# Sharing the last split weights between two passes, and moving low parts of weights from GpSimd to VectorE, in a two-block float32 model kernel

## The chip, the cores and the metric

The kernel runs on one core of one Trainium2 chip. The metric is the device time of one launch in microseconds. The kernel before the change took 1829.82 us, the median of three runs (1828.95 to 1830.59). PE is the matmul engine, DVE is VectorE, ACT is ScalarE, POOL is GpSimd, and SP is the engine whose queue starts most DMAs.

## The reference

All tensors are float32; x has 256 tokens of width 1024, and so has a second sequence, ctx. A first block (chunked retention and a gated linear recurrence) makes a new x. A second block has two layers, and in layer 0 both x and ctx go through nearly all of it, with the same weights:

```python
for l in range(DEPTH_2):                        # 2 layers
    h  = modulate(rms_norm_2(x,  g_pre_mix[l]), sh1, sc1)
    hc = modulate(rms_norm_2(xc, g_pre_mix[l]), csh1, csc1)
    (mq, ..., aq, ak, av, nq, nk, nv, zg) = split(h @ w_in[l])      # and the same of hc
    y_ml = mlstm_branch(...)                    # both sequences
    y_ga = gqa_latent(rope(rms(q_a)), rope(rms(k_a)), v_a, kc_a, vc_a)
    y_na = na_latent(...)                       # window attention
    o = merge_branches(y_ml, y_ga, y_na, zg, w_branch[l], w_out[l])
    x = x + ga1 * rms_norm_2(o, g_post_mix[l])
    f = conv_ffn(modulate(rms_norm_2(x, g_pre_ffn[l]), sh2, sc2), w_up[l], conv_w[l], conv_b[l], w_down[l])
    x = x + ga2 * rms_norm_2(f, g_post_ffn[l])
    if not last:                                # the same for xc, with the same weights
        ...
```

## The kernel before

**Products.** Matrix products have float32 accuracy from three products of rounded parts. A weight chunk of 128x1024 (512 KB) is loaded by SP into a buffer `wr` (L104), ACT casts it to its high part `wh` (L106), and DVE, or GpSimd where the caller names it with `eng`, subtracts to get the low part `wl` (L107). There are four buffers of each kind. Then `mm3` (L123 to L125) issues three matmuls for each tile: high by high, high by low, low by high. The activations are split likewise, into `hh` and `hl` for the normalized input of a layer. The accumulators lie in PSUM: four banks with tag `g`, two with tag `t` (names `psg`, `pst`), two more for scores.

**Normalization and put.** `post` adds the normalized output of a product to the residue (L1163). `norm_scale` then has ACT sum the squares (L269), DVE computes the reciprocal root in tiny steps of 128x2 (`rstd`: L247 to L261) and scales both halves of the tokens (L272, into `o` or `u`). `put_h` and `norm_put` have PE transpose the result in 128x128 pieces (L283, sixteen in all, in four banks' worth through two banks), after which DVE and ACT apply gain and shift and split the result into `hh` and `hl` (L297 to L302).

**Order.** Each engine executes its instructions in an order that the tile scheduler settles before the launch, from the order of the program and the buffers. An instruction that waits holds everything behind it on its engine. Two sequences, x (s = 0) and ctx (s = 1), share the weights of layer 0, but in three places the kernel makes two passes over a weight, one for each sequence, so that one pass's products run while the other sequence is normalized:

- The attention `gqa` of layer 0: `keys` (w_akv, two chunks, a pass is 48 matmuls of 128x256) and `queries` (w_aq, four chunks, 48 matmuls of 128x512), for ctx (k1, q1) and for x (k0, q0). q1 calls the put of x before its last chunk. After the products each stage normalizes its heads (`heads`, `query_heads`; L760 to L791) on DVE. A list named `order` says in which sequence the stages are issued. `behind` issues a stage after the put of x.
- w_o of layer 0, in `out_proj`: the last weight is gone over for x, then `between()` normalizes x, then it is gone over for ctx. Behind it, `put_h` for x, `post(1)` for ctx, the first four up-weights (`up_w`), and `put_h` for ctx.
- w_dn of layer 0, also in `out_proj`: 22 row blocks, six chunks of 128x1024 at most, a pass is 132 matmuls. The ctx pass calls the put of x among its products, before its last two chunks.

In each of these the second pass loads, casts and splits its chunks again, and their low parts are made by GpSimd. The other uses of `eng` are in the first block.

Of the kernel before, what the change touches and what calls it, by code (L numbers as in the profile page):

```python
# [72 lines left out]
class Kern:  # L73
# [70 lines left out]
            except StopIteration as e:  # L144
                return e.value

    def gemm_tok(self, src, x, seqs, order=None, eng=None, among=None):


        pss = {s: self.bank("g", 4).rearrange("p (t c) -> p t c", t=2) for s in seqs}  # L150
        nk = src.shape[-1] // 256
        order = order or list(range(0, nk, 4))
        done = 0
        for i, k0 in enumerate(order):
            if among and i + among[0] == len(order):
                among[1]()
            hi, lo = self.weights(src[:, k0 * 256 : min(nk, k0 + 4) * 256], eng)
            hi = hi.rearrange("p (k c) -> p k c", c=256)
            lo = lo.rearrange("p (k c) -> p k c", c=256)
            m = hi.shape[1]  # L160
            for s in seqs:
                for t in range(2):
                    for j in range(m):
                        r = slice(s * T + t * P, s * T + (t + 1) * P)
                        self.mm3(pss[s][:, t], x(k0 + j, r), (hi[:, j], lo[:, j]), done + j + t == 0, done + j + 1 == nk and t == 1)
            done += m
        return pss

    def gemm_wide(self, src, x, seqs, order=None, eng=None, at=None):


        while self.cur:
            self.step()
        pss = {s: [self.bank("g", 4) for _ in range(2)] for s in seqs}
        nk = src.shape[-1] // 512
        order = order or list(range(0, nk, 2))
        for i, k0 in enumerate(order):
            if at and i in at:
                at[i]()
            hi, lo = (a.rearrange("p (k c) -> p k c", c=512) for a in self.weights(src[:, k0 * 512 : (k0 + 2) * 512], eng))  # L180
            for s in seqs:
                for t in range(2):
                    for j in range(2):
                        r = slice(s * T + t * P, s * T + (t + 1) * P)
                        self.mm3(pss[s][t], x(k0 + j, r), (hi[:, j], lo[:, j]), i + j == 0, i + 1 == len(order) and j == 1)
        return pss
# [546 lines left out]
    def gqa(self, l, qs, fills):  # L733
        nc, A = self.nc, self.A
        y = self.new_y(len(qs) * T)
        with ExitStack() as es:
# [73 lines left out]
            vt, qT = {}, {}  # L810
            kT = [self.tl(gp, [P, 2, 512], "akT", 2, F32R) for _ in range(2)]

            def keys(qs):
                pss = self.gemm_tok(A[f"w_akv{l}"][0], self.h, qs, eng=nc.gpsimd if l == 0 else None)
                split = {}
                yield
                for s in qs:
                    vt[s] = self.tl(gp, [P, 2, P], "av", 2)
                    nc.scalar.copy(vt[s], pss[s][:, :, P:T])
                for s, k in zip(qs, heads([pss[s][:, :, 0:P] for s in qs], 2, qs, 1)):  # L820
                    ks = split[s] = self.tl(gp, [P, 8, 2, 64], "hs", 3, F32R).rearrange("p (h a) c f -> p h (a c) f", a=2)
                    for c in range(2):
                        nc.scalar.copy(ks[:, :, c], k)
                    for c in range(2):
                        nc.vector.tensor_tensor(ks[:, :, 2 + c], k, ks[:, :, c].bitcast(F32), ALU.subtract)
                yield
                for s, ks in split.items():
                    for kv in range(2):
                        pt = self.bank("t", 2)
                        for c in range(2):  # L830
                            for tt in range(2):
                                src = ks[:, 2 * tt + kv, 2 * c : 2 * c + 2].bitcast(F32).rearrange("p c f -> p (c f)")
                                nc.tensor.transpose(pt[:, c * T + tt * P : c * T + (tt + 1) * P], src, self.idn)

                        nc.scalar.copy(kT[kv][:, :, s * T : (s + 1) * T], pt.rearrange("p (c t) -> p c t", c=2))
                yield

            def queries(s, among=None):
                pss = self.gemm_wide(A[f"w_aq{l}"][0], self.h, (s,), eng=nc.gpsimd if l == 0 else None, at=among)[s]
                sts = []  # L840
                yield
                for q in query_heads((s, pss)):
                    st = self.tl(gp, [P, 8, 2, 64], "hs", 3, F32R)
                    nc.scalar.copy(st[:, :, 0], q)
                    nc.vector.tensor_tensor(st[:, :, 1], q, st[:, :, 0].bitcast(F32), ALU.subtract)
                    sts.append(st)
                yield
                for pr in range(4):
                    pt = self.bank("t", 2)
                    for j in range(2):  # L850
                        for tt in range(2):
                            src = sts[tt][:, 2 * pr + j].bitcast(F32).rearrange("p c f -> p (c f)")
                            nc.tensor.transpose(pt[:, j * T + tt * P : j * T + (tt + 1) * P], src, self.idn)
                    qT[s, pr] = self.tl(gp, [P, 2, T], "aqT", 4 * len(qs), F32R)
                    nc.scalar.copy(qT[s, pr].rearrange("p c t -> p (c t)"), pt)
                yield


            def put(ys, s):
                self.low = self.put_h(ys, l, 0, s)  # L860
                yield

            def behind(stage):
                with self.tc.issue_after(self.low):
                    next(stage)
                yield

            def fill(us):
                self.fill(us)
                yield  # L870

            if l == 0:
                k1, q1, k0, q0 = keys((1,)), queries(1, {3: lambda: next(put(self.yx, 0))}), keys((0,)), queries(0)
                order = (k1, q1, k0, behind(k1), q1, k1, q0, k0, q1, q0, k0, fill(fills[0]), q0)
            else:
                q0, k = queries(0), keys((0, 1))
                order = (q0, put(self.yc, 1), fill(2.5), q0, k, q0, k, fill(fills[0]), k)
# [305 lines left out]

    def out_proj(self, ws, x, qs, put, between, **among):

        c = 0
        for g, (w, n) in enumerate(ws):
            gemm = self.gemm_wide if n == 512 else self.gemm_tok
            cs = slice(c, c + n)
            c += n  # L1190
            pss = gemm(w, x, qs[:1] if g + 1 == len(ws) else qs)
            for s in pss:
                put(pss[s], s, g, cs)
        between()
        if len(qs) > 1:
            put(gemm(w, x, (1,), eng=self.nc.gpsimd, **among)[1], 1, g, cs)

    def layer(self, l, qs, out):
        nc, A, tc = self.nc, self.A, self.tc
# [2 lines left out]
        with ExitStack() as es:  # L1202
# [37 lines left out]
            f = FILLS[l]  # L1240
# [25 lines left out]
            def post(s):  # L1266
# [3 lines left out]
                self.norm_scale(xs, pp, ys)  # L1270
                return ys

            def take(ps, s, g, c):
                self.take(ps, o[s], ss[s], l, 0, s, g, c)
                self.fetch([w for w in late if not w.loaded][: 6 if l else 3])

            n = {}
            self.out_proj(
                [(A[f"w_o{l}"][g], 512) for g in range(2)],
                lambda kt, r: (mh[:, kt, r], ml[:, kt, r]),  # L1280
                qs,
# [13 lines left out]
                nc.vector.scalar_tensor_tensor(u3[:, :, 1:], p3[:, :, : T - 1], cw[:, 0, n : n + 1], u3[:, :, 1:], ALU.mult, ALU.add)  # L1295
                nc.vector.scalar_tensor_tensor(u3[:, :, : T - 1], p3[:, :, 1:], cw[:, 2, n : n + 1], u3[:, :, : T - 1], ALU.mult, ALU.add)  # L1296

            def up_w(n, eng=None):
                return self.weights(A[f"w_up{l}"][n], eng)

            def new_u():
                u = self.tl(self.up, [P, 1024], "u", 2)
# [3 lines left out]
            if len(qs) > 1:  # L1306
                rest, self.fillers = self.fillers, late
                self.fill(1.0)
                self.put_h(n[0], l, 1, 0)
                yc = post(1)  # L1310
                for i in range(2):
                    us = new_u()
                    ws = [up_w(i, nc.gpsimd), up_w(22 + i, nc.gpsimd)]
                    for j in range(2):
                        up(ws[j], i + 22 * j, us[j], 0, T)
                    ahead[i] = (us, ws)
                self.drain()
                self.fillers += rest
                self.put_h(yc, l, 1, 1)
            else:  # L1320
                self.fillers += late + self.tail
                while any(not w.done for w in late):
                    self.step()
                self.put_h(n[0], l, 1, 0)
        with ExitStack() as es:
# [42 lines left out]
            put = lambda ps, s, g, c: self.take(ps, f[s], ss[s], l, 1, s, g, c)  # L1368
            ws = [(A[f"w_dw{l}"][0], 512)] + [(A[f"w_dn{l}"][g], T) for g in range(2)]
            if l == 0:  # L1370
                self.out_proj(ws, x, qs, put, lambda: n.update({0: post(0, self.xd[0])}), among=(2, lambda: self.put_h(n[0], 1, 0, 0)))
                self.yc = post(1, None)
            else:
                self.out_proj(ws[:2], x, qs, put, lambda: None)
                self.finish(pp, A[f"w_dn{l}"][1], x, f[0], ss[0], res(0), out, l)
# [116 lines left out]
```

## Time and profile before

| | us |
|---|---|
| median of three runs | 1829.82 (1828.95 to 1830.59) |
| the profiled execution | 1827.0 |
| its span | 1825.2 |
| PE busy | 1750.8 (96%) |
| DVE busy | 1157.2 (63%) |
| ACT busy | 857.8 (47%) |
| POOL busy | 251.3 (14%) |
| granted TensorE clock, mean | 0.986 |

The rows are in microseconds from the start of the span. A row of a timeline has a start, a duration, the engine, the line, the operation with its output and inputs, and a count where neighbours of one kind are put together; the bracket holds the idle time just before it on its engine and what ended that. Durations of pipelined matmuls overlap, so their spacing is read from their starts. The clock of a stretch is a share of full speed.

### The profile page before, as it was taken

To read this page: it belongs to the slowest core of one execution; us is meant where nothing else is said; L and a number is where in the kernel's file an instruction comes from. 1 tells how busy PE (TensorE), PEld (TensorE's weight loads), DVE (VectorE), ACT (ScalarE), POOL (GpSimd) and SP (SyncE) were. 2 spreads that over 40 slices of the span, in tenths; PEclk is the share of its full clock that TensorE was granted. 3 is DMA by queue.
4 is the path that set the end of the run, shared out by engine and by line. 5 is a ranking of instruction groups with operands and counts; after the bars stand their busy time and mean duration, and the time that the engine had idled before them with its cause. 6 is when DMAs were issued, how large, how long until landed. Compare 5 with 4: busy or idle time off the path is not lost. (4 is left out here: it accounts for less than half of the span.)

```text
span 1825.2 us, 28352 instructions
## 1 busy us (share of the span) xinstructions
PE 1750.8 (96%) x10776; PEld 1491.0 (82%) x10776; DVE 1157.2 (63%) x2288; ACT 857.8 (47%) x1562; POOL 251.3 (14%) x182
## 2 busy tenths in 40 slices
PE   7998987999999999998999999998999999999998
PEld 6888876777888877786877888898998987679998
DVE  7888858445434678557656564249664459768874
ACT  5463343444534545434534442235655445456652
POOL 2213042000101021003110110021001012002210
PEclk9999999999999999998999999999999999999999
DMA  8863453566534342374354324344554644576563
GB/s 304 283 204 121 136 173 109 195 205 194 191 98 156 85 130 87 132 249 161 128 185 141 102 93 134 100 142 148 166 176 148 230 128 129 202 272 200 185 222 112
DMA packets 112825, 299.11 MB, mean 164 GB/s; under 512 B 28305, under 2 KB 38609, under 8 KB 112433
## 3 DMA queue, kind: packets, MB, share of 16 engines
q1 hardware_dynamic: 111984, 296.37, 50.0%
q8 instruction: 85, 1.39, 0.3%
q10 hardware_dynamic: 432, 0.57, 0.1%
q0 software_dynamic: 272, 0.36, 0.1%
q14 instruction: 52, 0.42, 0.1%
HBM read 281.46 MB, written 19.46 MB: 165 GB/s over the span
## 5 line engine op out<-in xcount | busy, mean ns | idle before, releaser
L107 DVE TENSOR_TENSOR wl<-wr,wh 128x1024 fp32r<-128x1024 f32 (+1 forms) x333 | 412.0, 1239 | 350.2 <-ACT wh L106 343.0
L106 ACT CAST wh<-wr 128x1024 fp32r<-128x1024 f32 x368 | 382.6, 1041 | 454.3 <-PE psg L125 173.5
L123 PE MATMUL psg<-hh,wh 128*128 128x256 f32 (+1 forms) x1712 | 570.8, 335 | 0.5 <-ACT hh L298 0.5
L124 PE MATMUL psg<-hl,wh 128*128 128x256 f32 (+1 forms) x1712 | 565.9, 331 | 0.0
L125 PE MATMUL psg<-hh,wl 128*128 128x256 f32 (+1 forms) x1712 | 564.1, 330 | 0.0
L123 PEld LDWEIGHTS psg<-hh,wh 128*128 128x128 f32 x1712 | 326.8, 191 | 46.9 <-issue 11.5
L125 PEld LDWEIGHTS psg<-hh,wl 128*128 128x128 f32 x1712 | 327.4, 191 | 30.0 <-issue 0.8
L124 PEld LDWEIGHTS psg<-hl,wh 128*128 128x128 f32 x1712 | 327.4, 191 | 27.7 <-DVE hl L292 0.2
L107 POOL TENSOR_TENSOR wl<-wr,wh 128x1024 fp32r<-128x1024 f32 (+1 forms) x35 | 82.5, 2367 | 352.8 <-ACT wh L106 352.4
L123 PE MATMUL psg<-wh,hh 128*128 128x512 f32 (+1 forms) x320 | 120.6, 377 | 7.4 <-DVE p L767 5.3
L125 PE MATMUL psg<-wh,hl 128*128 128x512 f32 (+1 forms) x320 | 119.9, 375 | 2.1 <-DVE hl L302 2.1
L124 PE MATMUL psg<-wl,hh 128*128 128x512 f32 (+1 forms) x320 | 119.7, 374 | 0.0
L1340 POOL TENSOR_TENSOR u<-u 128x512 f32<-128x512 f32 (+1 forms) x44 | 61.1, 1389 | 412.7 <-DVE u L1296 412.7
L123 PE MATMUL psg<-wh,midh 128*128 128x256 f32 (+1 forms) x364 | 117.7, 323 | 0.0
L124 PE MATMUL psg<-wl,midh 128*128 128x256 f32 (+1 forms) x364 | 117.6, 323 | 0.0
L125 PE MATMUL psg<-wh,midl 128*128 128x256 f32 (+1 forms) x364 | 117.4, 322 | 0.0
L123 PEld LDWEIGHTS psg<-wh,hh 128*128 128x128 f32 x320 | 61.2, 191 | 17.9 <-DVE p L767 5.5
L123 PEld LDWEIGHTS psg<-wh,midh 128*128 128x128 f32 x364 | 69.8, 192 | 5.2
L124 PEld LDWEIGHTS psg<-wl,midh 128*128 128x128 f32 x364 | 69.7, 192 | 5.2
L683 ACT ACTIVATE p<-pss,sm 128x512 f32<-128x512 f32 x64 | 44.0, 687 | 63.7 <-DVE sm L682 63.5
L125 PEld LDWEIGHTS psg<-wh,midl 128*128 128x128 f32 x364 | 69.7, 192 | 5.1
L125 PEld LDWEIGHTS psg<-wh,hl 128*128 128x128 f32 x320 | 61.2, 191 | 12.5 <-DVE hl L302 2.5
(305 smaller groups left out, 2705.4 us busy)
## 6 DMA issues: line engine op xcount, KB each, us to landing
wr<-in_w_up_dram SPq DMA_DIRECT2D x88, 512.0 KB, 3.6
wr<-in_w_mod_dram SPq DMA_DIRECT2D x55, 512.0 KB, 4.0
wr<-in_w_zg_dram SPq DMA_DIRECT2D x48, 512.0 KB, 4.2
wr<-in_w_in_dram SPq DMA_DIRECT2D x40, 512.0 KB, 4.4
wr<-in_w_dn_dram SPq DMA_DIRECT2D x25, 512.0 KB, 3.8
wr<-in_w_br_dram SPq DMA_DIRECT2D x24, 512.0 KB, 3.6
wr<-in_w_dw_dram SPq DMA_DIRECT2D x22, 512.0 KB, 3.4
wr<-in_w_o_dram SPq DMA_DIRECT2D x20, 512.0 KB, 5.4
```

Source lines behind the costliest of these rows:

```text
L106: nc.scalar.copy(hi, raw)
L107: self.last_lo = (eng or nc.vector).tensor_tensor(lo, raw, hi.bitcast(F32), ALU.subtract).ins
L123: mm(ps, a[0], b[0], start=first, stop=False)
L124: mm(ps, a[0], b[1], start=False, stop=False)
L125: mm(ps, a[1], b[0], start=False, stop=last)
L683: nc.scalar.activation(t, s, AF.Exp, bias=m, accum_out=z)
L1340: nc.gpsimd.tensor_tensor(a, a, b, ALU.mult)
```

## The change

`parts` remembers the split parts of a chunk, and `again` gives the last ones of a pass, with the order of chunks reversed, for the next pass. Three passes use them: k0 takes both chunks of k1; q0 begins with the last two chunks of q1 and loads the other two; the ctx passes over w_o and w_dn begin with the last four chunks of the x passes, which is all of w_o, and load two of w_dn. `eng` is gone from `gemm_tok`, `gemm_wide` and `up_w`: their low parts are all made by DVE. The order of the stages in `gqa` changes, with the put of x behind the products of q1 and k1; in `out_proj` of w_o, `between()` comes behind the second pass in the program, and the take of ctx's part (`rest_put`) behind the put of x; in w_dn the put of x comes before the last chunk instead of before the last two.

```diff
@@ -144,7 +144,20 @@
             except StopIteration as e:
                 return e.value
 
-    def gemm_tok(self, src, x, seqs, order=None, eng=None, among=None):
+    def parts(self, parts, k0, src):
+
+        parts = {} if parts is None else parts
+        if k0 not in parts:
+            parts[k0] = self.weights(src)
+        return parts[k0]
+
+    @staticmethod
+    def again(parts, n=4):
+
+        ks = list(parts)[::-1]
+        return {k: parts[k] for k in ks[:n]}, ks
+
+    def gemm_tok(self, src, x, seqs, order=None, among=None, parts=None):
 
 
         pss = {s: self.bank("g", 4).rearrange("p (t c) -> p t c", t=2) for s in seqs}
@@ -154,7 +167,7 @@
         for i, k0 in enumerate(order):
             if among and i + among[0] == len(order):
                 among[1]()
-            hi, lo = self.weights(src[:, k0 * 256 : min(nk, k0 + 4) * 256], eng)
+            hi, lo = self.parts(parts, k0, src[:, k0 * 256 : min(nk, k0 + 4) * 256])
             hi = hi.rearrange("p (k c) -> p k c", c=256)
             lo = lo.rearrange("p (k c) -> p k c", c=256)
             m = hi.shape[1]
@@ -166,7 +179,7 @@
             done += m
         return pss
 
-    def gemm_wide(self, src, x, seqs, order=None, eng=None, at=None):
+    def gemm_wide(self, src, x, seqs, order=None, at=None, parts=None):
 
 
         while self.cur:
@@ -177,7 +190,7 @@
         for i, k0 in enumerate(order):
             if at and i in at:
                 at[i]()
-            hi, lo = (a.rearrange("p (k c) -> p k c", c=512) for a in self.weights(src[:, k0 * 512 : (k0 + 2) * 512], eng))
+            hi, lo = (a.rearrange("p (k c) -> p k c", c=512) for a in self.parts(parts, k0, src[:, k0 * 512 : (k0 + 2) * 512]))
             for s in seqs:
                 for t in range(2):
                     for j in range(2):
@@ -810,8 +823,8 @@
             vt, qT = {}, {}
             kT = [self.tl(gp, [P, 2, 512], "akT", 2, F32R) for _ in range(2)]
 
-            def keys(qs):
-                pss = self.gemm_tok(A[f"w_akv{l}"][0], self.h, qs, eng=nc.gpsimd if l == 0 else None)
+            def keys(qs, parts=None):
+                pss = self.gemm_tok(A[f"w_akv{l}"][0], self.h, qs, parts=parts)
                 split = {}
                 yield
                 for s in qs:
@@ -835,8 +848,9 @@
                         nc.scalar.copy(kT[kv][:, :, s * T : (s + 1) * T], pt.rearrange("p (c t) -> p c t", c=2))
                 yield
 
-            def queries(s, among=None):
-                pss = self.gemm_wide(A[f"w_aq{l}"][0], self.h, (s,), eng=nc.gpsimd if l == 0 else None, at=among)[s]
+            def queries(s, parts=None, order=None):
+                parts, order = self.again(*order) if order else (parts, None)
+                pss = self.gemm_wide(A[f"w_aq{l}"][0], self.h, (s,), order=order, parts=parts)[s]
                 sts = []
                 yield
                 for q in query_heads((s, pss)):
@@ -870,8 +884,9 @@
                 yield
 
             if l == 0:
-                k1, q1, k0, q0 = keys((1,)), queries(1, {3: lambda: next(put(self.yx, 0))}), keys((0,)), queries(0)
-                order = (k1, q1, k0, behind(k1), q1, k1, q0, k0, q1, q0, k0, fill(fills[0]), q0)
+                pk, pq = {}, {}
+                q1, k1, k0, q0 = queries(1, pq), keys((1,), pk), keys((0,), pk), queries(0, None, (pq, 2))
+                order = (q1, k1, put(self.yx, 0), k0, behind(q1), behind(k1), q0, k1, k0, q1, q0, k0, fill(fills[0]), q0)
             else:
                 q0, k = queries(0), keys((0, 1))
                 order = (q0, put(self.yc, 1), fill(2.5), q0, k, q0, k, fill(fills[0]), k)
@@ -1183,17 +1198,25 @@
 
     def out_proj(self, ws, x, qs, put, between, **among):
 
+
+        parts = {}
         c = 0
         for g, (w, n) in enumerate(ws):
             gemm = self.gemm_wide if n == 512 else self.gemm_tok
             cs = slice(c, c + n)
             c += n
-            pss = gemm(w, x, qs[:1] if g + 1 == len(ws) else qs)
+            last = g + 1 == len(ws)
+            pss = gemm(w, x, qs[:1] if last else qs, parts=parts if last else None)
             for s in pss:
                 put(pss[s], s, g, cs)
-        between()
+        if among:
+            between()
         if len(qs) > 1:
-            put(gemm(w, x, (1,), eng=self.nc.gpsimd, **among)[1], 1, g, cs)
+            parts, order = self.again(parts)
+            pss = gemm(w, x, (1,), order=order, parts=parts, **among)
+        if not among:
+            between()
+        return lambda: put(pss[1], 1, g, cs)
 
     def layer(self, l, qs, out):
         nc, A, tc = self.nc, self.A, self.tc
@@ -1270,12 +1293,13 @@
                 self.norm_scale(xs, pp, ys)
                 return ys
 
+
             def take(ps, s, g, c):
                 self.take(ps, o[s], ss[s], l, 0, s, g, c)
                 self.fetch([w for w in late if not w.loaded][: 6 if l else 3])
 
             n = {}
-            self.out_proj(
+            rest_put = self.out_proj(
                 [(A[f"w_o{l}"][g], 512) for g in range(2)],
                 lambda kt, r: (mh[:, kt, r], ml[:, kt, r]),
                 qs,
@@ -1295,8 +1319,8 @@
                 nc.vector.scalar_tensor_tensor(u3[:, :, 1:], p3[:, :, : T - 1], cw[:, 0, n : n + 1], u3[:, :, 1:], ALU.mult, ALU.add)
                 nc.vector.scalar_tensor_tensor(u3[:, :, : T - 1], p3[:, :, 1:], cw[:, 2, n : n + 1], u3[:, :, : T - 1], ALU.mult, ALU.add)
 
-            def up_w(n, eng=None):
-                return self.weights(A[f"w_up{l}"][n], eng)
+            def up_w(n):
+                return self.weights(A[f"w_up{l}"][n])
 
             def new_u():
                 u = self.tl(self.up, [P, 1024], "u", 2)
@@ -1307,10 +1331,11 @@
                 rest, self.fillers = self.fillers, late
                 self.fill(1.0)
                 self.put_h(n[0], l, 1, 0)
+                rest_put()
                 yc = post(1)
                 for i in range(2):
                     us = new_u()
-                    ws = [up_w(i, nc.gpsimd), up_w(22 + i, nc.gpsimd)]
+                    ws = [up_w(i), up_w(22 + i)]
                     for j in range(2):
                         up(ws[j], i + 22 * j, us[j], 0, T)
                     ahead[i] = (us, ws)
@@ -1368,7 +1393,7 @@
             put = lambda ps, s, g, c: self.take(ps, f[s], ss[s], l, 1, s, g, c)
             ws = [(A[f"w_dw{l}"][0], 512)] + [(A[f"w_dn{l}"][g], T) for g in range(2)]
             if l == 0:
-                self.out_proj(ws, x, qs, put, lambda: n.update({0: post(0, self.xd[0])}), among=(2, lambda: self.put_h(n[0], 1, 0, 0)))
+                self.out_proj(ws, x, qs, put, lambda: n.update({0: post(0, self.xd[0])}), among=(1, lambda: self.put_h(n[0], 1, 0, 0)))()
                 self.yc = post(1, None)
             else:
                 self.out_proj(ws[:2], x, qs, put, lambda: None)
```

The instruction lists differ in these three places alone. Loads on SP from 661 rows to 649, casts on ACT from 1332 rows to 1320, rows of POOL from 174 to 148; 14 rows with L107 more on DVE.

SP, in the attention of layer 0, the loads of w_akv and w_aq before the change:

```order
L104 DMA wr_2853<-in_w_akv_dram 128x1024
L104 DMA wr_2883<-in_w_akv_dram 128x1024
L104 DMA wr_2915<-in_w_aq_dram 128x1024
L104 DMA wr_2933<-in_w_aq_dram 128x1024
L104 DMA wr_2951<-in_w_aq_dram 128x1024
L104 DMA wr_3021<-in_w_aq_dram 128x1024
L104 DMA wr_3040<-in_w_akv_dram 128x1024
L104 DMA wr_3070<-in_w_akv_dram 128x1024
L104 DMA wr_3178<-in_w_aq_dram 128x1024
```

and after it:

```order
L104 DMA wr_2854<-in_w_aq_dram 128x1024
L104 DMA wr_2872<-in_w_aq_dram 128x1024
L104 DMA wr_2890<-in_w_aq_dram 128x1024
L104 DMA wr_2908<-in_w_aq_dram 128x1024
L104 DMA wr_2927<-in_w_akv_dram 128x1024
L104 DMA wr_2957<-in_w_akv_dram 128x1024
L104 DMA wr_3178<-in_w_aq_dram 128x1024
L104 DMA wr_3196<-in_w_aq_dram 128x1024
```

The four chunks of q1 now come ahead of the two of k1, k0 loads nothing, and the two chunks that q0 loads (3178, 3196) follow at once; before, six loads of w_aq and w_akv stood behind the first two.

DVE, at w_o of layer 0, between the residue of x (L1163 before, L1178 after) and its scaling (L272 before, L285 after); before:

```order
L1163 SCALAR_TENSOR_TENSOR res_7932<-o_1507_7696,prs_7936,res_7932 128x1024
L1163 SCALAR_TENSOR_TENSOR res_7934<-o_1507_7696,prs_7936,res_7934 128x1024
L247 TENSOR_SCALAR rstd_1555_7965<-nss_7961 128x2
L248 TENSOR_SCALAR rstd_1557_7967<-rstd_1555_7965 128x2
L249 TENSOR_SCALAR rstd_1557_7967<-rstd_1557_7967 128x2
L259 SCALAR_TENSOR_TENSOR rstd_1556_7966<-rstd_1557_7967,rstd_1555_7965 128x1 x2
```

and after:

```order
L1178 SCALAR_TENSOR_TENSOR res_7958<-o_1495_7672,prs_7962,res_7958 128x1024
L1178 SCALAR_TENSOR_TENSOR res_7960<-o_1495_7672,prs_7962,res_7960 128x1024
L107 TENSOR_TENSOR wl_8139<-wr_8136,wh_8138 128x1024
L107 TENSOR_TENSOR wl_8145<-wr_8142,wh_8144 128x1024
L260 TENSOR_SCALAR rstd_1545_7991<-nss_7987 128x2
L261 TENSOR_SCALAR rstd_1547_7993<-rstd_1545_7991 128x2
L262 TENSOR_SCALAR rstd_1547_7993<-rstd_1547_7993 128x2
L272 SCALAR_TENSOR_TENSOR rstd_1546_7992<-rstd_1547_7993,rstd_1545_7991 128x1 x2
```

Two low parts of weights stand ahead of the reciprocal root; one more (wl_8208) stands further on, just ahead of the root's last step of 128x1.

PE, at w_dn of layer 0, where the transposes of x (L283 before, L296 after) stand in the ctx pass; before, with the chunk wh_11182 ahead of them and wh_11264 behind:

```order
L123 MATMUL psg_11089<-wh_11182,midh_9729 128x256
L124 MATMUL psg_11089<-wl_11183,midh_9729 128x256
L125 MATMUL psg_11089<-wh_11182,midl_9730 128x256
L283 MATMUL pst_11210<-idn,o_1905_10198 128x128 x4
L283 MATMUL pst_11223<-idn,o_1905_10198 128x128 x4
L123 MATMUL psg_11089<-wh_11264,midh_9806 128x256
```

and after, with wh_11128 ahead and wh_11210 behind:

```order
L123 MATMUL psg_11041<-wh_11128,midh_9032 128x256
L124 MATMUL psg_11041<-wl_11129,midh_9032 128x256
L125 MATMUL psg_11041<-wh_11128,midl_9033 128x256
L296 MATMUL pst_11156<-idn,o_1881_10150 128x128 x4
L296 MATMUL pst_11169<-idn,o_1881_10150 128x128 x4
L123 MATMUL psg_11041<-wh_11210,midh_8417 128x256
```

In the ctx pass 108 of the 132 matmuls stand ahead of the transposes, and 96 before the change; the chunks come in falling order (row block 8417 belongs to the first chunk of the weight, 9806 to the last but one).

## Rows read from the trace of the kernel before

**Rows 1.** The page's first part: busy us, share of the span, instructions.

```profile
PE 1750.8 (96%) x10776; PEld 1491.0 (82%) x10776; DVE 1157.2 (63%) x2288; ACT 857.8 (47%) x1562; POOL 251.3 (14%) x182
```

**Rows 2.** Four stretches: busy us of each engine, clock, DMA share, GB/s.

```profile
240.00:320.00 80.00, 65.56 (x340) 53.82 (x339) 60.02 (x138) 34.50 (x59) 35.27 (x25) 0.91 0.42 133
320.00:790.00 470.00, 469.48 (x2567) 369.83 (x2566) 262.06 (x525) 217.42 (x483) 36.90 (x26) 1.00 0.48 151
790.00:890.00 100.00, 90.58 (x538) 76.34 (x537) 66.87 (x142) 45.73 (x82) 21.49 (x10) 0.95 0.49 164
...
1190.00:1300.00 110.00, 100.58 (x750) 96.50 (x749) 78.09 (x190) 57.02 (x108) 20.75 (x19) 0.95 0.49 154
```

**Rows 3.** Timeline of PE, attention of layer 0.

```profile
249.23 0.28 PE L123 MATMUL psg<-wh,hh 128*128 128x256 f32 x1
...
254.99 0.40 PE L123 MATMUL psg<-wh,hh 128*128 128x512 f32 x1
...
268.13 2.32 PE L283 MATMUL pst<-idn,u 128*128 128x128 f32 x8 [4.80 <-DVE u L272]
...
290.02 0.80 PE L123 MATMUL psg<-wh,hh 128*128 128x512 f32 x1 [5.31 <-DVE p L767]
```

**Rows 4.** Timeline of PE, w_o of layer 0 and behind it.

```profile
845.99 0.47 PE L283 MATMUL pst<-idn,o 128*128 128x128 f32 x1 [8.29 <-DVE o L272]
...
865.93 1.22 PE L283 MATMUL pst<-idn,o 128*128 128x128 f32 x8
```

**Rows 5.** Timeline of PE, w_dn of layer 0.

```profile
1231.95 2.33 PE L283 MATMUL pst<-idn,o 128*128 128x128 f32 x8 [3.90 <-DVE o L272]
```

**Rows 6.** Timeline of DVE, w_o of layer 0 and behind it.

```profile
827.15 2.42 DVE L248 TENSOR_SCALAR rstd<-rstd 128x2 int32<-128x2 int32 x1
829.60 2.32 DVE L249 TENSOR_SCALAR rstd<-rstd 128x2 int32<-128x2 int32 x1
...
837.81 1.38 DVE L247 TENSOR_SCALAR rstd<-nss 128x2 f32<-128x2 f32 x1 [2.01 <-ACT o L269]
...
841.52 2.27 DVE L249 TENSOR_SCALAR rstd<-rstd 128x2 int32<-128x2 int32 x1
...
859.58 0.17 DVE L248 TENSOR_SCALAR rstd<-rstd 128x2 int32<-128x2 int32 x1
...
872.29 0.43 DVE L302 TENSOR_TENSOR hl<-fs,hh 128x256 fp32r<-128x256 f32 x1 [0.45 <-ACT hh L301]
```

**Rows 7.** Timeline of POOL, w_o of layer 0.

```profile
827.14 4.75 POOL L107 TENSOR_TENSOR wl<-wr,wh 128x1024 fp32r<-128x1024 f32 x2 [0.90 <-ACT wh L106]
```

**Rows 8.** Timeline of DVE, attention of layer 0.

```profile
251.97 1.48 DVE L247 TENSOR_SCALAR rstd<-nss 128x2 f32<-128x2 f32 x1 [1.85 <-ACT u L623]
...
263.36 2.27 DVE L248 TENSOR_SCALAR rstd<-rstd 128x2 int32<-128x2 int32 x1
...
270.96 0.41 DVE L302 TENSOR_TENSOR hl<-fs,hh 128x256 fp32r<-128x256 f32 x1
...
280.47 2.37 DVE L302 TENSOR_TENSOR hl<-fs,hh 128x256 fp32r<-128x256 f32 x1 [1.25 <-ACT hh L301]
...
289.88 0.68 DVE L791 TENSOR_REDUCE hss<-p 128x8 f32<-128x512 f32 x1
```

**Rows 9.** Timeline of POOL, attention of layer 0.

```profile
251.02 4.89 POOL L107 TENSOR_TENSOR wl<-wr,wh 128x1024 fp32r<-128x1024 f32 x2 [0.71 <-ACT wh L106]
...
270.40 1.08 POOL L748 TENSOR_TENSOR rot<-rope,gqk 128x32 f32<-128x32 f32 x4
```

**Rows 10.** Timeline of DVE, w_dn of layer 0.

```profile
1218.73 2.34 DVE L248 TENSOR_SCALAR rstd<-rstd 128x2 int32<-128x2 int32 x1
```

**Rows 11.** The page's costliest groups, L107 and L106: count, busy us, mean ns, idle before.

```profile
L107 DVE TENSOR_TENSOR wl<-wr,wh 128x1024 fp32r<-128x1024 f32 (+1 forms) x333 | 412.0, 1239 | 350.2 <-ACT wh L106 343.0
L106 ACT CAST wh<-wr 128x1024 fp32r<-128x1024 f32 x368 | 382.6, 1041 | 454.3 <-PE psg L125 173.5
...
L107 POOL TENSOR_TENSOR wl<-wr,wh 128x1024 fp32r<-128x1024 f32 (+1 forms) x35 | 82.5, 2367 | 352.8 <-ACT wh L106 352.4
```

## The prediction

> **What bounds the kernel now.** The page's first part comes first: PE is busy for 1750.8 of 1825.2 us [rows 1]. So the kernel can only gain in the 74 us in which PE stands still, or where PE runs at its lower clock. The busy time of each engine in stretches shows where that is: 320 to 790, say, is full (469.48 of 470, clock 1.00), while 240 to 320 lacks 14.4 us, 790 to 890 lacks 9.4 and 1190 to 1300 lacks 9.4, with a clock of 0.91, 0.95 and 0.95 [rows 2]. These are the three places that the diff touches: A, the first attention of layer 0; B, its w_o; C, its w_dn.
>
> PE's timeline gives the waits. In A it stands 4.80 us before eight transposes at 268.13 and 5.31 us before q0's first product at 290.02 [rows 3]; in B 8.29 us before 845.99 [rows 4]; in C 3.90 us before 1231.95 [rows 5]. DVE releases each of them, with the last step of a normalization. After a wait of 4.80 or 3.90 us the eight transposes take 2.32 and 2.33 us, while the eight at 865.93, with no long wait before them, take 1.22: PE is then at 1.2 GHz instead of 2.4 [rows 3, 4, 5].
>
> DVE's timeline says why DVE is late. A shift of 128x2 integers takes 0.17 us at 859.58, but 2.42 at 827.15 [rows 6]. GpSimd then runs two low parts from 827.14 on, 4.75 us together [rows 7], that is to 831.89; DVE's two tiny steps (2.42, and 2.32 at 829.60) end at 831.92. In A the step at 251.97 + 1.48 lies within GpSimd's 251.02 + 4.89 [rows 8, 9], and a low part of 128x256, 0.43 at 872.29, takes 2.37 at 280.47 [rows 6, 8]. So a DVE instruction that meets a low part on GpSimd stands until that ends. Taking 0.17 (0.43 for a low part of 128x256) for each slow step: in B five steps, the first at 827.15 and the last at 841.52, lose 9.8 us; in C three around 1218.73 [rows 10] lose 4.7; in A four before the transposes, the first at 251.97 and the last at 263.36, lose 6.75, and those behind, 280.47 among them, some 9.8 more. Together about 31 us of DVE's time, mostly on the way to PE's waits.
>
> **The change part by part.** *Weights.* Twelve loads, twelve casts of 1.04 us on ACT and 26 low parts of 2.37 us on GpSimd go; 14 low parts of 1.24 us come to DVE (8 in A, 4 in B, 2 in C) [rows 11]. The loads and casts that go are worth nothing by themselves: no wait above ends with a DMA or a cast, and ACT is busy 34.5 of 80, 45.7 of 100 and 57.0 of 110 us there [rows 2]. What they cost in return is that kept parts hold their wh and wl buffers (four each), so that the next chunk's cast, and DVE's low part behind it, can begin only when a shared chunk has been used for the last time. That is in the sums below.
>
> *A.* PE now does q1 and k1 whole before the transposes: 48 products of 128x512 spaced by 0.23 us (before, 36 of them lie from 254.99 to the wait that begins at 263.33; 11.0 for 48) and 48 of 128x256 spaced by 0.12 (from 249.23 to 254.99; 5.8), together from 249.2 to 266.0 [rows 3]. The normalized x was ready at 268.0, just before PE's 268.13. Less the 6.75 us of stalls, plus one low part (wl_2930) inside the chain (1.24) and 0.4 for one that delays the sum before it, it is ready near 263. So the wait of 4.80 goes, the transposes start 2.1 us earlier, and 12 more products (2.7) are done by then. From transposes to the last low part of h takes 6.8 us where nothing disturbs it (865.93 to 872.7) [rows 4, 6]; one weight's cast and low part stand in it now, 2.5 more: the last is ready at 275.3, not 282.8. q0's first product needs banks that q1's results hold until their heads have been taken from them, and by the order these come behind the last low part of h: two reductions of 0.68 [rows 8], twelve small steps of about 0.2 (as the rows of 0.16 and 0.17), a weight of 1.24 and the first product by the norm (0.69 for 512 columns by my estimate from the 0.68 of the reduction), 5.8 together. q0 starts at 281.1 instead of 290.0: **8.9 gained**, with a new wait of some 4 us in place of the 5.31. Bounds: 5.9 if only the first wait and the clock after it (4.8 + 1.1) are won; 13 if q0 starts right behind k0, near 277.
>
> *B.* The 9.8 us of stalls go. Two of the new low parts, wl_8139 and wl_8145, stand where DVE waits 2.01 us for ACT's squares [rows 6] and cost 0.5 at most; wl_8208 stands in the chain (1.24). o, ready at 846.0, comes at 838.0 to 838.7. PE's last product before it ends at 845.99 - 8.29 = 837.7, so the wait shrinks from 8.3 to some 0.6 (7.7), and the slow clock after it goes (1.1). Behind it the take of ctx's half now stands after the first put of h; it, ctx's normalization and four low parts (5.0) then fill DVE, and the second transposes, at 865.93 before [rows 4], wait 1.3 us by my estimate, so that 7.7 + 1.1 - 1.3 remain and they come at 858.4: **7.5 gained**; bounds 4 (that second wait as long as the four low parts, 5) and 9.5 (no such wait).
>
> *C.* The 4.7 us go; wl_11129 and wl_11211, and a part of the next stage's first, add 2.1. o is ready near 1229.4 instead of 1232. PE, which reached the put at 1231.95 - 3.90 = 1228.05, now has 12 more products of 0.12 before it (1.4) and arrives at 1229.5. It waits 0.4 at most; 12 products fewer remain behind, and the clock is not lost: 2.05 (1231.95 against 1229.9) + 1.44 (products done by then) + 1.9 (1.1 for the transposes, 0.8 for the products after them, an estimate) = **5.4 gained**; bounds 2 (only 24 instead of 36 products are left to cover the low parts of h, and PE waits for them) and 6.
>
> *Sum.* 8.9 + 7.5 + 5.4 = 21.8. Behind each place the order is as before and PE full, as in 320 to 790 [rows 2], so nothing is there to take it back. The profiled execution took 1827.0 us, 1.8 more than its span; it becomes 1805.2. The median of the three runs, 1829.82, lies 2.8 above it, so I predict **1808.0**. The bounds alone sum to 11.9 and 28.5, that is 1818 and 1801.
>
> **One rule against it.** GpSimd keeps its ten steps for the rotation in A, the last four 1.08 us from 270.40 [rows 9]. A low part of h with two inputs at 270.96 ran beside them in 0.41 us, as undisturbed [rows 6, 8]. I cost them at nothing. The Trainium skill (SBUF — State Buffer, "Who interferes with whom") says that a VectorE instruction with two SBUF inputs contends with any GpSimd instruction that reads SBUF, by an exclusive lock that the first to start holds to its end. By that rule the trace should show a loss at 270.96 and it does not; for the 2.40 us low parts of GpSimd it agrees.
>
> **The rivals.** *Rotation blocks (the rule's case).* If the ten steps of some 0.27 us (1.08 by 4) did hold DVE while it makes the low parts of h, now that these come sooner, A loses up to 2.8: 1810.8. For it: the long steps show such a block. Against: the 0.41.
>
> *Half of it.* DVE becomes the engine that all three places wait for: 14 low parts of 1.24 are 17.4 us, and my sum puts only some 8 of them on a path. If the rest lies there too (9), or the kept buffers delay casts by as much, the gain is 12 to 13: 1817. For it: DVE ended every wait before. Against: it is busy 60 of 80, 67 of 100, 78 of 110 us [rows 2], and the 31 us of stalls are in these.
>
> *More.* The heads of q1 and the second put of B find their inputs in time: the three upper bounds, 28.5, and one or two us of clock: 1799.
>
> *Nothing reaches the end.* What A to C win is lost where a later stage waits for a load that the earlier start brings no sooner: 1829 to 1830. Against: DMA share 0.42 to 0.49 [rows 2], and no wait shown ends with a load.
>
> *Slower.* The long tiny steps are not GpSimd's doing but DVE's own (a late input that is counted as busy). Then the stalls stay, and the low parts in the chains are added: 5.3 in A (1.24 + 0.4 + 2.5 + 1.24), 3.7 in B, 2.5 in C, 11.5 in all: about 1841. The point from which this decides: if less than about 11.5 of the 31 us of stalls go. Against: ends that agree to 0.03 us at 831.9.
>
> **How the numbers follow.** Forecast 0.59 (its own range 1802 to 1814), rule's case 0.04, half 0.17, more 0.07, nothing 0.07, slower 0.06. To leave out no more than 2 in 10 the range takes most of the half case and none of the other three: 1800 to 1822. A measurement of this kernel tells 0.2%, 3.7 us, from no change (1826.2 to 1833.5): faster 0.87, same 0.07, slower 0.06.
>
> **What would show it.** In the new profile: GpSimd's low parts fall from 35 to 9, DVE's rise from 333 to 347 and ACT's casts fall from 368 to 356; no tiny DVE step over 0.5 us in the three places; no wait before A's first transposes, about 4 us before q0, under 1 in B and in C before the first transposes, 1 to 2 before B's second; the eight transposes in 1.2 us. The forecast is wrong if the tiny steps stay long, or if they are short and the four long waits of PE, 22.3 us before, still sum to over 14.

## The result, and the profile after

The changed kernel took 1802.98 us, the median of four runs (1801.03 to 1805.59), against 1830.01 of the kernel before (four runs, 1828.95 to 1830.59): 27.0 us less, a ratio of 0.9856 with an interval of 0.9844 to 0.9869. The forecast was 1808.0, the range 1800 to 1822. The profiled execution took 1805.59 us (span 1803.8), the highest of the four.

The page and the groups of the changed kernel, to hold against [rows 1, 11]:

```profile
PE 1747.8 (97%) x10776; PEld 1487.2 (82%) x10776; DVE 1139.7 (63%) x2302; ACT 847.6 (47%) x1550; POOL 192.7 (11%) x156
...
L107 DVE TENSOR_TENSOR wl<-wr,wh 128x1024 fp32r<-128x1024 f32 x347 | 428.6, 1237 | 351.8 <-ACT wh L106 341.2
L106 ACT CAST wh<-wr 128x1024 fp32r<-128x1024 f32 x356 | 370.9, 1043 | 442.6 <-PE psg L125 175.1
```

DVE makes 14 low parts more, 16.6 us by this group (428.6 against 412.0), and yet is busy 17.5 us less (1157.2 before): some 34 us went in which it was counted as busy and stood, where the prediction had 31. The stretches, with the columns of [rows 2], moved to where the same work now lies:

```profile
240.00:312.00 72.00, 66.52 (x364) 55.34 (x363) 54.86 (x149) 34.84 (x60) 6.31 (x13) 0.98 0.39 123
...
779.00:875.00 96.00, 93.65 (x545) 77.82 (x544) 63.15 (x150) 43.68 (x79) 3.43 (x2) 0.98 0.45 153
...
1175.00:1280.00 105.00, 99.59 (x767) 95.17 (x766) 77.22 (x196) 55.30 (x108) 7.49 (x13) 1.00 0.45 147
```

PE lacks 5.5, 2.4 and 5.4 us there (14.4, 9.4 and 9.4 before). PE's timeline at the four long waits of [rows 3 to 5]:

```profile
252.75 0.39 PE L123 MATMUL psg<-wh,hh 128*128 128x512 f32 x1
...
269.38 1.03 PE L296 MATMUL pst<-idn,u 128*128 128x128 f32 x8
...
283.63 0.50 PE L123 MATMUL psg<-wh,hh 128*128 128x512 f32 x1 [3.62 <-DVE p L808]
...
828.42 1.46 PE L296 MATMUL pst<-idn,o 128*128 128x128 f32 x8
...
849.22 0.33 PE L296 MATMUL pst<-idn,o 128*128 128x128 f32 x1 [0.93 <-DVE o L285]
849.88 1.19 PE L296 MATMUL pst<-idn,o 128*128 128x128 f32 x7 [0.33 <-DVE o L285]
851.68 1.22 PE L123 MATMUL psg<-hh,wh 128*128 128x256 f32 x4 [0.61 <-ACT hh L311]
...
1214.65 1.30 PE L296 MATMUL pst<-idn,o 128*128 128x128 f32 x8
```

No bracket stands at 269.38, 828.42 and 1214.65: the waits of 4.80, 8.29 and 3.90 us are gone, and the transposes take 1.0 to 1.5 us instead of 2.3. Before q0 a wait of 3.62 has taken the place of 5.31. DVE's steps at w_o, for [rows 6]:

```profile
817.93 0.17 DVE L261 TENSOR_SCALAR rstd<-rstd 128x2 int32<-128x2 int32 x1
818.13 0.17 DVE L262 TENSOR_SCALAR rstd<-rstd 128x2 int32<-128x2 int32 x1
```

0.17 us, where 2.42 and 2.32 stood.

**Where the time came from.** The same instruction in both traces gives the offset of after against before. The table has the change of that offset over each place: first block up to the attention's first product; A up to the take of x at w_o; B up to the first product of 128x512 behind it; C from the take at w_dn to the first product of 128x256 behind the 128x512 ones that follow; and the rest.

| us, against the trace of before | first block | A | B | C | rest |
|---|---|---|---|---|---|
| changed kernel | +3.5 | -12.7 | -5.5 | -5.7 | -1.0 |
| the same, profiled again | +0.6 | -12.6 | -6.7 | -5.7 | -0.9 |
| A alone | +1.3 | -13.1 | -0.3 | -0.4 | -0.6 |
| B alone | +0.6 | +1.4 | -5.4 | +0.7 | -1.1 |
| C alone | +1.0 | +0.2 | -0.1 | -5.7 | +1.0 |
| only moved to DVE | +0.1 | -12.4 | -8.6 | -5.7 | +1.5 |
| shared, on GpSimd | +0.3 | -7.5 | -1.2 | -0.4 | +1.5 |
| dummy reads | +2.8 | -12.6 | +1.3 | -5.7 | +0.5 |
| dummy writes | +0.5 | -11.1 | -6.0 | -5.7 | -0.3 |
| heads first | +0.5 | -14.6 | -6.7 | -5.7 | +1.3 |
| moved, first block too | -15.1 | -12.1 | -8.6 | -5.6 | +2.9 |
| gate row, heads, first block | -12.8 | -15.0 | -9.95 | -5.7 | -0.9 |
| w_o unshared, heads, first block | -15.1 | -14.2 | -8.6 | -5.7 | -0.7 |

(Where the take at w_o has no idle time before it, which is so in the kernels with w_o unshared and all on DVE, its second row is used.) Untouched places move by up to 1.5 us from run to run, the rest by up to 2.9, the first block by up to 3.5.

### The profile page after: what moved, and what is told of

It reads as the page before. It is cut to its first block, busy times and chain, and to the rows that moved or that the text cites. A ratio compares the mean times of both kernels' runs of the same rounds, so it can differ in the third digit from the quotient of the medians.

```text
span 1803.8 us, 28275 instructions
## 1 busy us (share of the span) xinstructions
PE 1747.8 (97%) x10776; PEld 1487.2 (82%) x10776; DVE 1139.7 (63%) x2302; ACT 847.6 (47%) x1550; POOL 192.7 (11%) x156
## 5 line engine op out<-in xcount | busy, mean ns | idle before, releaser
L107 DVE TENSOR_TENSOR wl<-wr,wh 128x1024 fp32r<-128x1024 f32 x347 | 428.6, 1237 | 351.8 <-ACT wh L106 341.2
L106 ACT CAST wh<-wr 128x1024 fp32r<-128x1024 f32 x356 | 370.9, 1043 | 442.6 <-PE psg L125 175.1
L123 PEld LDWEIGHTS psg<-hh,wh 128*128 128x128 f32 x1712 | 328.0, 192 | 47.2 <-issue 11.9
L1316 ACT ACTIVATE u<-psg,prm 128x256 f32<-128x256 f32 (+1 forms) x92 | 59.8, 650 | 25.1 <-PE psg L125 25.0
```

Source lines behind the costliest of these rows:

```text
L106: nc.scalar.copy(hi, raw)
L107: self.last_lo = (eng or nc.vector).tensor_tensor(lo, raw, hi.bitcast(F32), ALU.subtract).ins
L123: mm(ps, a[0], b[0], start=first, stop=False)
L1316: nc.scalar.activation(u, ps, AF.Identity, scale=cw[:, 1, n : n + 1], bias=cb[:, n : n + 1])
```

## The experiments

**Each place alone.** Two of the three places are put back as they were.

> Only the attention of layer 0 (A) is changed; w_o, the up-weights and w_dn are as before. My theory (the gain arises place by place, where DVE's blocked steps and the order made PE wait): about 12.7 us less than before, as the two traces differ between the first product of the attention and the start of w_o, so 1817 (1815 to 1819). The rival (the gain comes from less traffic and fewer casts over the whole kernel, or the places need each other): well under half of that, 1824 or more.

> Only w_o of layer 0 and the first up-weights (B) are changed. My theory: 5.5 us less than before, 1824.5 (1823 to 1826.5), with a tail at the lower clock behind the second transposes. The rival: no clear difference alone, 1828 to 1831.

> Only w_dn of layer 0 (C) is changed. My theory: 6 us less than before, 1824 (1822.5 to 1825.5), and the wait of 3.90 us before the transposes gone. The rival: no clear difference alone, 1828 to 1831.

Measured: 1814.2 (ratio 0.9921, 0.9904 to 0.9938), 1822.49 (0.9963, 0.9951 to 0.9974) and 1822.96 (0.9969, 0.9958 to 0.9981), against 1829.7. The three gains, 15.5, 7.2 and 6.7, are each 0.7 to 2.8 us larger than expected; by the ratios they sum to 1.47%, and the whole change gives 1.44%. So the places are independent as far as these runs tell, and the rival of a gain spread over the kernel falls.

**What in a place does it: moving, or sharing?** The kernel before with the argument `eng` left out in the second block, and nothing else:

```diff
-pss = self.gemm_tok(A[f"w_akv{l}"][0], self.h, qs, eng=nc.gpsimd if l == 0 else None)
+pss = self.gemm_tok(A[f"w_akv{l}"][0], self.h, qs)
```

(and so in `queries`, `out_proj` and for the first up-weights).

> The kernel before with nothing shared and no order changed; only the 26 low parts of the three places are made by DVE instead of GpSimd. If the block by GpSimd is what costs (my theory), the stalls of 31 us go and 26 low parts of 1.24 come, part of them beside waits: 6 to 14 us less, 1816 to 1824. If the sharing and the order make the gain (rival), DVE only has more to do: 1828 to 1840.

Measured: 1801.9 (1800.89 to 1805.87), ratio 0.9855 (0.9836 to 0.9873). That is the whole gain, with all twelve loads and casts still there, the order of before, and 26 instead of 14 low parts on DVE. It is more than I had expected (6 to 14). DVE's low parts take 29.0 us more (441.0 against 412.0) and DVE is busy 1153.0, 4.2 us less: some 33 us of standing went. Why the 26 cost PE so little is not shown; at w_o three of them stand in the chain to x's transposes. The opposite: the changed kernel with `eng=nc.gpsimd` given back to the 14.

> The changed kernel, sharing and order kept, but the 14 low parts that it still makes in the three places are given back to GpSimd. My theory (a low part on GpSimd blocks DVE's small steps): steps of 1 to 2.4 us return in all three places and the kernel loses 8 to 18 us, 1811 to 1821. The rival (sharing and order made the gain): within 3 us of the changed kernel, 1802 to 1806.

Measured: 1817.85 (1815.24 to 1819.73), ratio 0.9928 (0.9908 to 0.9949): 15 us of the 27 are lost again, in all three places (table). With the low parts on GpSimd, sharing and the new order together gain 12 us, and leave 14 of the 26 there; on top of the move they are worth nothing that these runs can tell.

**Is it GpSimd's access that blocks DVE?** Of the engines' lists only POOL's differs from the changed kernel's:

```diff
...
+nc.gpsimd.tensor_copy(J[:, 0:4], ss[0].rearrange("p a b -> p (a b)"))
+for _ in range(7):
+    nc.gpsimd.tensor_tensor(J, J, J, ALU.add)
...
```

> The changed kernel with extra work on GpSimd alone: at w_o, once the sums of squares of x are there, seven additions of a 128x512 tile of zeros to itself that nobody else uses. All other engines' lists are as in the changed kernel. If GpSimd's reading of SBUF blocks DVE (my theory): DVE's tiny steps behind 817 take up to 1.4 us each, o comes 6 to 9 us later, PE waits 5 to 8 us before the first transposes: 1809 to 1814. If DVE's long steps had another cause (rival): no change, 1802 to 1806.

Measured: 1809.82 (1808.61 to 1813.16), 6.8 us more than the changed kernel. POOL, DVE and PE of this run:

```profile
816.68 7.77 POOL L1309 TENSOR_TENSOR junk<-junk 128x512 f32<-128x512 f32 x7
```

```profile
817.98 0.89 DVE L262 TENSOR_SCALAR rstd<-rstd 128x2 int32<-128x2 int32 x1
818.91 1.20 DVE L272 SCALAR_TENSOR_TENSOR rstd<-rstd,rstd 128x1 f32<-128x1 f32 x2
820.03 1.07 DVE L274 SCALAR_TENSOR_TENSOR rstd<-rstd,rstd 128x1 f32<-128x1 f32 x2
```

```profile
832.91 0.48 PE L296 MATMUL pst<-idn,o 128*128 128x128 f32 x1 [5.06 <-DVE o L285]
```

Steps that take 0.15 to 0.2 us undisturbed take up to one addition of GpSimd (1.11) while these run, and PE's wait is back. The rival that DVE's steps are long by themselves is out at w_o. With writes alone, twelve `memset` of the tile in place of the additions:

> As the run with the additions, but GpSimd writes zeros to the tile twelve times and reads nothing. If only reading (the shared read port) blocks DVE: no change, 1802 to 1806, and tiny steps of 0.17 us beside the writes. If any GpSimd access to SBUF blocks DVE: steps of the length of a write, and 3 to 8 us more.

```profile
815.92 6.95 POOL L1309 MEMSET junk<- 128x512 f32 x12
```

```profile
816.55 0.50 DVE L261 TENSOR_SCALAR rstd<-rstd 128x2 int32<-128x2 int32 x1
817.08 0.55 DVE L262 TENSOR_SCALAR rstd<-rstd 128x2 int32<-128x2 int32 x1
817.67 0.35 DVE L272 SCALAR_TENSOR_TENSOR rstd<-rstd,rstd 128x1 f32<-128x1 f32 x2
```

Measured: 1804.07 (1801.58 to 1805.56), not told from the changed kernel. The steps of 128x1 with two inputs are not touched by writes; the two integer steps are, by up to one write (0.58). My "tiny steps of 0.17 us beside the writes" was a miss by these two.

**The new waits.** q1's heads ahead of the put of x:

```diff
-order = (q1, k1, put(self.yx, 0), k0, behind(q1), behind(k1), q0, ...
+order = (q1, k1, q1, put(self.yx, 0), k0, behind(k1), q0, ...
```

> The changed kernel with q1's heads taken ahead of the put of x in the attention, in the 3.7 us in which DVE waits for the first transposes. If the wait of 3.62 us before q0 is set by the chain of heads behind the low parts of h (my reading): the wait before q0 goes, the low parts of h come some 3 us later, together 1 to 3 us less than the changed kernel. If the low parts of h are what PE needs first (rival): 0 to 3 us more.

Measured: 1802.49 (1800.9 to 1803.59), not told from the changed kernel; the 1 to 3 us are not seen in the whole. In A the offset of the one execution is 1.9 us better: the wait before q0 is gone, one of 4.17 us for the first parts of h stands before k0's products, and q0 begins earlier. The last four runs share a chip (before: 1828.36):

> The changed kernel itself, on the same chip as the three beside it: 1801 to 1806. By place (offsets against the trace of before): attention 12.7 us, w_o 5.5, w_dn 5.7; the first block, which is unchanged, varies by up to 3.5 us from run to run.

Measured: 1802.75 (1801.57 to 1803.09), ratio 0.9854 (0.984 to 0.9868).

> The kernel before with nothing shared, and the low parts of the three places (26) and of the retention's gates in the first block (8) on DVE; one low part at the very start stays on GpSimd. If a low part on GpSimd blocks DVE there too (steps of 1.43 to 2.50 us between 147 and 185 in the trace of before), the waits of PE at 160, 167 and 172 us shrink: 2 to 7 us less than the run that moved the 26 alone (1801.9), 1795 to 1800. If DVE is simply full there (rival): no change or up to 4 us more, 1801 to 1806.

```diff
-sg = gate(24 + h, nc.gpsimd)
+sg = gate(24 + h)
...
```

(and the edits of the move above). Measured: 1787.86 (1785.45 to 1789.64), ratio 0.9773 (0.9758 to 0.9789): 14 us less than moving the 26 alone, twice my upper bound. The stretch 140 to 190, in which PE lacked 9.5 us before, at a clock of 0.90, before and in this run:

```profile
140.00:190.00 50.00, 40.46 (x289) 39.08 (x288) 40.48 (x117) 16.56 (x30) 19.01 (x8) 0.90 0.36 117
```

```profile
140.00:190.00 50.00, 49.77 (x396) 48.47 (x395) 45.30 (x170) 22.18 (x39) 0.00 (x0) 1.00 0.50 148
```

A step of the retention before, at 153.02, with the step ahead of it and GpSimd's row, and the same step in this run:

```profile
152.57 0.42 DVE L552 SCALAR_TENSOR_TENSOR sg<-sg,psg 128x256 f32<-128x256 f32 x1 [0.81 <-ACT sg L307]
153.02 2.00 DVE L562 SCALAR_TENSOR_TENSOR y<-sg,mh 128x256 f32<-128x256 f32 x1
```

```profile
152.33 2.40 POOL L107 TENSOR_TENSOR wl<-wr,wh 128x1024 fp32r<-128x1024 f32 x1 [2.54 <-ACT wh L106]
```

```profile
151.54 0.42 DVE L562 SCALAR_TENSOR_TENSOR y<-sg,mh 128x256 f32<-128x256 f32 x1
```

I had counted three waits of PE (2.03, 0.96 and 3.40) and left out a fourth (3.15 at 185.96) and the clock: at 0.90 it costs another 5 of 50 us by estimate, and the first block gained 15.1. Each of the eight low parts there held up one step of DVE. That any DVE instruction which meets a low part stands until its end, as the prediction says, is too wide: `sg<-sg,psg`, with one input in PSUM, took 0.42 beside the low part and 0.41 without one.

> The changed kernel with q1's heads ahead of the put, with the low parts of the first block's gates on DVE, and with the gate row for ctx's take in a buffer of its own, loaded at the start of w_o. The last edit is read at w_o alone: if the take of ctx's half comes late because its gate row waits for a shared buffer until 836 and DVE then stands 2.9 us idle (my reading), w_o gains some 3 us more than in the changed kernel, 8.5 instead of 5.5. If the order of the second pass itself costs (rival), it stays at 5.5. In all 1791 to 1798.

```diff
...
+own[1, 1] = self.gate_row(0, 0, 1, c1, self.tl(pp, [P, 512], "grow"))
...
```

Measured: 1781.76 (1780.14 to 1783.26), ratio 0.9741 (0.9726 to 0.9755), the fastest kernel of this study. At w_o, where of its edits only the gate row counts, it gains 9.95 us, as my reading had it (8.5) and more. The gate row's start and DVE around the take in the changed kernel, and the take in this one:

```profile
835.95 0.33 SPq L1154 DMA_DIRECT2D fs<-gd  x1
```

```profile
840.32 0.48 DVE L1319 SCALAR_TENSOR_TENSOR u<-psg,prm,u 128x255 f32<-128x255 f32 x1 [2.93 <-ACT u L1316]
840.72 1.28 DVE L1166 TENSOR_TENSOR o<-psg,fs 128x512 f32<-128x512 f32 x2
```

```profile
810.11 1.28 DVE L1166 TENSOR_TENSOR o<-psg,grow 128x512 f32<-128x512 f32 x2
```

The take stood 11.9 us behind the last scaling of x (828.84); now it follows it at once.

> As the run with the gate row, but w_o as before the change (two passes that share nothing, normalization of x between them), its low parts on DVE, and no buffer for the gate row. At w_o it should gain 8.6 us, as in the run that only moved the low parts; the attention 14.6, w_dn 5.7. In all 1791 to 1798, within 2 us of the run with the gate row.

Measured: 1783.37 (1781.7 to 1785.03), ratio 0.975 (0.9735 to 0.9765); w_o gains 8.6. So w_o without any sharing is some 2 to 3 us better than shared, unless the gate row has its own buffer. Both totals lie 8 to 9 us under the range that I wrote, by the first block (12.8 and 15.1 gained there).

## Why the prediction was right, point by point

- *GpSimd's low parts block DVE, and that makes PE wait*: shown at w_o by the dummy reads, which add GpSimd's work and nothing else; in A and C by the move alone, with the steps of DVE that end where GpSimd's end. That GpSimd's slower low parts (2.37 us for 1.24) came late for PE is a rival that no run tests alone; no wait of PE shown ends with one.
- *Loads and casts are worth nothing*: shown; the run that keeps all twelve takes 1801.9.
- *A, 8.9*: mis-sized, 12.7. q0 began 6.39 + 3.52 = 9.9 us earlier, with a wait of 3.62 where I had some 4. The other 2.8 lie behind q0, where I had taken the order to be as before and counted nothing: before, PE waited three times more between 308 and 321 for heads:

```profile
308.24 0.44 PE L833 MATMUL pst<-idn,hs 128*128 128x128 f32 x2 [0.51 <-ACT hs L823]
...
319.01 0.41 PE L853 MATMUL pst<-idn,hs 128*128 128x128 f32 x2 [1.49 <-DVE hs L845]
...
320.90 0.88 PE L853 MATMUL pst<-idn,hs 128*128 128x128 f32 x6 [0.31 <-DVE hs L845]
```

  In the changed kernel these waits, 2.3 us of the 2.8, are absent. And the order that I gave credit for (q1 and k1 whole before the put) was not needed: the move alone gives 12.4.
- *B, 7.5*: the second transposes came 16.71 us earlier than before, 7.5 of them won here, as forecast. The step that failed stands behind them, where by the prediction nothing was to take it back: 2.0 us went, after waits of 0.93, 0.33 and 0.61, with a clock of 0.65 in 852 to 856. In the second profile of the same kernel, with the same waits, it stayed at 1.00, 0.8 went and B gained 6.7; so it did with the heads first, while B alone had these waits and the low clock (0.59 in 863 to 867). So some 1.2 us are the clock's; what decides it is open. The reason that I gave for the second wait was wrong too: DVE was not full behind the first put but stood 2.93 us, with the late take behind. With the take early B gains 9.95, above my upper bound of 9.5.
- *C, 5.4*: 5.7.
- *Sum, 21.8 for the profile*: 21.4, but as 12.7 + 5.5 + 5.7 + 1.0 less 3.5 in the unchanged first block, where this execution waited 1.59 us at 59.33 instead of 0.41 for DVE and then ran at the lower clock. So the agreement of the sums is partly chance; the median moved by 27.0.
- *Rivals*: "slower", "nothing" and "half" are out. The time lies between the forecast and "more". The rotation steps ran from 266.55 to 269.1, while DVE waited 3.69 us for the transposes: they met nothing, so the rule's case did not arise. But the prediction read only DVE's side of it. In the trace of before, the last of the ten steps starts while the low part of h (270.96 to 271.37) runs:

```profile
271.04 0.44 POOL L748 TENSOR_TENSOR rot<-rope,gqk 128x32 f32<-128x32 f32 x1
```

  and four of them in the changed kernel:

```profile
268.23 0.88 POOL L761 TENSOR_TENSOR rot<-rope,gqk 128x32 f32<-128x32 f32 x4
```

  It takes 0.44 (0.45 in the two runs that keep the old attention beside a changed place) where the seven others of 128x32 take some 0.25, so that four took 1.08 for 0.88: here GpSimd, which came second, was held, as the rule says. The loss that the prediction did not find stood in GpSimd's row.

## What to carry to other kernels

A tiny instruction that takes several microseconds, and ends when an instruction of another engine ends, is a wait in disguise: compare each form's duration with its own undisturbed row before reading what it computes. Work given to GpSimd "for free" can be paid by VectorE's dependent chains, up to a whole GpSimd instruction for a small step; look at all such places, not only at those with a long wait behind them. Before a rearrangement is credited with a gain, undo everything but its smallest part.

## What the runs showed of the hardware that was not expected

A GpSimd write without inputs (0.58 us) held up integer steps of 128x2 on DVE (0.50 and 0.55 for 0.17), but not two-input steps of 128x1 (0.35 for two); GpSimd additions (1.11 us) held up both. Beside a low part on GpSimd (2.40 us) a step of DVE with one input in PSUM took its usual 0.42 us, while one with both in SBUF took 2.00. GpSimd can be the one that is held: a rotation step that began beside a low part of h on DVE took 0.44 for 0.25. And a granted clock of 1.00 or 0.65 was seen in two executions of one kernel, in the 4 us behind the same waits of PE.
